# Gate copies issued in quarters between U tiles, and one U tile split in every step

## The chip, the cores and the metric

The kernel runs on one core of one Trainium2 chip. The metric is device time in microseconds (us) of one launch; lower is better. TensorE is called PE here, VectorE DVE, ScalarE ACT, GpSimd POOL. SP (SyncE) computes nothing: it issues DMAs.

## The reference, cut to what matters

One residual block over 512 tokens of width 1024: a gated token mixer, then a retrieval layer (PEER), then a norm. The change lies in the kernel's PEER part:

```
def peer(xn, w_q, sub_keys, u_tab, v_tab):       # 512 tokens, 8 heads, 128 x 128 = 16384 experts
    ...                                          # two top-16 searches per head, then the best 16 of the sums:
    ...                                          # idx (expert numbers) and g (softmax gates), 128 per token
    def block(args):                             # 128 tokens at a time
        tb, ib, gb = args
        ue = u_tab[ib]
        act = jax.nn.gelu(jnp.einsum("phkd,pd->phk", ue, tb))
        ve = v_tab[ib]
        return jnp.einsum("phk,phkd->pd", gb * act, ve)
```

So each token meets 128 chosen rows of U and of V, each weighted by its gate.

## The kernel before, in words

The kernel runs in stages on one core: the input projection and the mixers (to about 330 us of the span), the queries and the top-16 searches (to about 580), the gates (to about 855) and a V stretch to the end.

For the first 128 tokens the kernel gathers the chosen rows of U and V. For the other three groups of 128 tokens (the index `t_` in the code, 0 to 2) it computes densely: all 16384 hidden values, each multiplied by its gate, which is zero for an expert not chosen. The experts are cut into 128 tiles of 128. A U tile is 512 KB: it is loaded to `raw`, split into a high part `hi` (ACT) and a low part `lo` (DVE), multiplied with the tokens' high and low parts in 24 matmuls (`h_mm`, L147 to L149), and put through gelu (`h_act`). Of the 128 U tiles, 60 are worked through before the V stretch, as company for other work; results for which there is no room are written to HBM.

The gates stage makes, for each group of 128 tokens, a table `stg` of 128 x 128 x 128 gates in SBUF. It takes eight steps a group (here s0 to s7; `s2` in the code). In each step `mid()` does, for two sets of eight tokens, the gate products on PE (`gate_mm`, 32 matmuls into four PSUM tiles, of which there are six), their eviction to `stg` on ACT (L731, four a step), and on DVE the one-hot operands of the next step (`one_hot`, L716 and L718, four operations a step). Around it, `h_step` carries one U tile along: it asks for a load, takes loaded tiles from the list `raws` and makes their `hi` ahead of `mid()` and their `lo` behind it, so that they join the list `nxt`; then it multiplies the first tile of `nxt` and evicts it. `nxt` holds at most three tiles (`SB`), `raws` six buffers (`RB`). The argument `splits` says how many tiles the step splits at most.

There is one `stg` buffer. Groups 0 and 1 are copied from it to the table `gd` in HBM, four DMAs of 2 MB on SP's queue, and `h_step` then runs six times without gates (here b0 to b5, `HB`). Group 2 stays in SBUF. After it the kernel multiplies the last tile that is split, and the V stretch begins.

The order of instructions on PE, DVE, ACT and POOL is that of the code here: `pinned()` ties each to the one before it on its engine. It does so for every engine but SP (L93), whose order is left to the scheduler of the framework.

Of the kernel before, what the change touches and what calls it, by code (L numbers as in the profile page):

```python
# [25 lines left out]
NDT = NTT - 1  # L26
# [15 lines left out]
HB = (6, 6, 0)  # L42
# [5 lines left out]
GSTEP = (1, 0, 0)  # L48
SB = 3
# [11 lines left out]
def tile_block(ctx: ExitStack, tc: tile.TileContext, x, w_in, vecs, w_ax, w_out, n2row, w_q, skT,  # L61
# [12 lines left out]
    def ps_b(name):  # L74
        return ps.tile([P, 512], F32, tag="b", name=name, bufs=6)
# [22 lines left out]
    def load(src, name, nsub=None):  # L98
        raw = strm.tile([P, D], F32, tag="raw", name=f"raw_{name}", bufs=RB)
        dst = raw if nsub is None else raw.rearrange("p (a b) -> p a b", a=nsub)  # L100
        sync.dma_start(dst, src)
        return raw

    def split(raw, name, lo_eng, pl=None):
        hi = (pl or strm).tile([P, D], F32R, tag="hi", name=f"hi_{name}", bufs=SB)
        lo = (pl or strm).tile([P, D], F32R, tag="lo", name=f"lo_{name}", bufs=SB)
        act.activation(hi, raw, AF.Copy)  # L107
        lo_eng.tensor_tensor(lo, raw, hi, op=ALU.subtract)  # L108
        return hi, lo
# [45 lines left out]
    with ExitStack() as fctx:  # L155
# [31 lines left out]
        with pinned():  # L187
# [5 lines left out]
            raws = [load(w_in[s_ * KD], f"in{s_}_0") for s_ in (0, 1, 4)]  # L193
# [182 lines left out]
    def drain(left):  # L376
        while len(dq) > left:
            dq.pop(0)()
# [44 lines left out]
    def flush():  # L423
        while pend:
            h_act(*pend.pop(0))

    def h_load():
        nonlocal hn
        if hn < nlag:
            raws.append((hord[hn], load(uT[hord[hn]], f"u{hord[hn]}")))  # L430
            hn += 1

    def h_split(pl=None, lo_eng=pool, most=3):
        here = sum(1 for e in nxt if e[2] is None)
        if here < most - (pl is not None):
            pl = None
        elif pl is None or len(nxt) - here >= 3:
            return
        if raws:
            i, raw = raws.pop(0)  # L440
            nxt.append((i, split(raw, f"u{i}", lo_eng, pl), pl))

    def h_run():
        if nxt:
            i, (hi, lo), _ = nxt.pop(0)
            pend.append((i, h_mm(i, hi, lo)))

    raws, nxt = [], []

    def h_turn(n, lo_eng=pool):  # L450
        for _ in range(n):
            if len(raws) < 2:
                h_load()
            h_run()
            h_split(lo_eng=lo_eng)
            flush()
# [215 lines left out]
    def gather_steps(n, left=0):  # L672
        while n > 0 and gpos[0] < len(gsched):
            f, a = gsched[gpos[0]]
            f(a)
            drain(left)
            gpos[0] += 1
            if f is not gather_w:
                n -= 1
# [3 lines left out]
    with ExitStack() as gctx:  # L683
        op = gctx.enter_context(tc.tile_pool(name="op", bufs=1))
        io = op.tile([P, P, 2], F16, name="io")
        pool.iota(io, pattern=[[1, P], [0, 2]], base=0, channel_multiplier=0, allow_small_or_imprecise_dtypes=True)
        h_turn(HPRO)
        pte = ps_b("pte")
        ptg = ps_b("ptg")
        for t in range(NDT):  # L690
            pe.transpose(pte[:, t * P:(t + 1) * P], eall[:, 1 + t, :], ident)
            pe.transpose(ptg[:, t * P:(t + 1) * P], gall[:, 1 + t, :], ident)
        ef = op.tile([P, TD], F32, name="ef")
        ij = op.tile([P, TD // OC, 2, OC], F16, name="ij")
        g12 = op.tile([P, TD // OC, 2, OC], F16, name="g12")

        def by_sub(tl):
            return tl[:, :TD].rearrange("p (s o) -> p s o", o=OC)


        dve.tensor_scalar(ef, pte[:, :TD], 1.0 / NKEY, -(NKEY - 1.0) / (2 * NKEY), op0=ALU.mult, op1=ALU.add)
        act.activation(g12[:, :, 0, :], by_sub(ptg), AF.Copy, scale=GSC)
        dve.tensor_scalar(ef, ef, ROUND, -ROUND, op0=ALU.add, op1=ALU.add)
        dve.scalar_tensor_tensor(ij[:, :, 1, :], by_sub(ef), -float(NKEY), by_sub(pte), op0=ALU.mult, op1=ALU.add)
        act.activation(ij[:, :, 0, :], by_sub(ef), AF.Copy)
        dve.scalar_tensor_tensor(g12[:, :, 1, :], by_sub(ptg), GSC, g12[:, :, 0, :], op0=ALU.mult, op1=ALU.subtract)

        iob = io.unsqueeze(1).to_broadcast([P, OC, P, 2])

        def one_hot(sub):  # L710
            def bc(tl):
                pairs = tl[:, sub].rearrange("p v (q b) -> p (v q) b", b=2)
                return pairs.unsqueeze(2).to_broadcast([P, OC, P, 2])

            oij, o12 = [op.tile([P, OC, P, 2], F16, tag=n, name=f"{n}_{sub}", bufs=OB) for n in ("oij", "o12")]
            dve.tensor_tensor(oij, iob, bc(ij), op=ALU.is_equal)  # L716
            oi = oij[:, :OC // 2].unsqueeze(1).to_broadcast([P, 2, OC // 2, P, 2])
            dve.tensor_tensor(o12.rearrange("p (v q) k b -> p v q k b", v=2), oi,  # L718
                              bc(g12).rearrange("p (v q) k b -> p v q k b", v=2), op=ALU.mult)
            return oij, o12  # L720

        def gate_mm(sub, oij, o12):
            for q4 in range(OC // 4):
                pg = ps_b(f"pg{sub}_{q4}")
                for t in range(4):
                    o = pg[:, t * P:(t + 1) * P]
                    q, b = divmod(q4 * 4 + t, 2)
                    pe.matmul(o, oij[:, OC // 2 + q, :, b], o12[:, q, :, b], start=True, stop=False)
                    pe.matmul(o, oij[:, OC // 2 + q, :, b], o12[:, OC // 2 + q, :, b], start=False, stop=True)
                tt = sub * OC % P + q4 * 4  # L730
                act.activation(stg[:, :, tt:tt + 4], pg.rearrange("p (t i) -> p i t", t=4), AF.Copy)  # L731

        def h_step(mid, splits=1):
            if len(raws) < RB:
                h_load()
            made = []
            while len(made) < splits and len(nxt) + len(made) < SB and raws:
                k_, raw = raws.pop(0)  # L740
                hi = strm.tile([P, D], F32R, tag="hi", name=f"hi_u{k_}", bufs=SB)
                act.activation(hi, raw, AF.Copy)  # L742
                made.append((k_, raw, hi))
            mid()
            for k_, raw, hi in made:
                lo = strm.tile([P, D], F32R, tag="lo", name=f"lo_u{k_}", bufs=SB)
                dve.tensor_tensor(lo, raw, hi, op=ALU.subtract)  # L747
                nxt.append((k_, (hi, lo), None))
            h_run()
            flush()  # L750

        NSUB = NDT * P // OC
        ohs = {u: one_hot(u) for u in range(OB)}
        h_turn(HPRO2, dve)
        for t_ in range(NDT):
            stg = sp.tile([P, P, P], F32, tag="stg", name=f"stg{t_}", bufs=1)
            for s2 in range(P // OC // 2):
                sub = t_ * (P // OC) + 2 * s2

                def mid():  # L760
                    for u in (sub, sub + 1):
                        gate_mm(u, *ohs.pop(u))
                    for u in (sub + OB, sub + OB + 1):
                        if u < NSUB:
                            ohs[u] = one_hot(u)

                if s2 >= 4 and len(raws) < RB:
                    h_load()

                h_step(mid, 0 if t_ and s2 < 2 else 2 if s2 in (4, 6) else 1)  # L770
                gather_steps(GSTEP[(sub // 2) % len(GSTEP)], 2)
            if t_ < NDT - 1:
                for q4 in range(4):
                    sl = slice(q4 * 32, (q4 + 1) * 32)
                    sync.dma_start(gd[sl, :, t_ * P:(t_ + 1) * P].rearrange("i j t -> j i t"), stg[:, sl, :])  # L775
            for m in range(HB[t_]):
                h_step(lambda: None)
        while nxt or raws:
            flush()
            h_split()  # L780
            h_run()
        drain(0)
        flush()
# [54 lines left out]
    for i in range(NKEY):  # L838
        raw = vr.pop(i) if i in vr else load(v_tab[i * P:(i + 1) * P, :], f"v{i}")
        hi, lo = split(raw, f"v{i}", dve)  # L840
# [79 lines left out]
```

## Time and profile before

| | us |
|---|---|
| median of 3 runs | 1696.33 (1694.04 to 1698.31) |
| the profiled execution | 1695.04 |
| its span, first to last instruction | 1693.3 |
| PE busy | 1627.9 (96%) |
| DVE busy | 1267.5 (75%) |
| ACT busy | 690.1 (41%) |
| granted PE clock, mean over the span | 0.98 |

Times within the profile are counted from the span's start. A row of idle time names what ended it. The clock is the share of full speed that was granted to PE. Busy time of an engine that is not the bottleneck costs nothing by itself.

### The profile page before, as it was taken

The numbers are of one execution on the slowest core, as the hardware profiler recorded it, in microseconds if no ns is written. First come the engines' busy times: TensorE is split into PE (matmuls) and PEld (weight loads), VectorE is DVE, ScalarE is ACT, GpSimd is POOL, SyncE is SP. The second block draws the span as 40 slices with busy tenths as digits, with TensorE's granted clock in tenths as the row PEclk, the third lists the DMA queues.
The fourth block names the chain that finished last, engine by engine and source line by source line (L and its number), as shares of the span: only waits on it lengthen the run. The fifth ranks groups of instructions, "written<-read, shape, count | busy, mean of one in ns | idle before, by whom it ended". The sixth has DMA issues, their size and how long they took to land.

```text
span 1693.3 us, 23571 instructions
## 1 busy us (share of the span) xinstructions
PE 1627.9 (96%) x8402; PEld 1429.3 (84%) x8402; DVE 1267.5 (75%) x2404; ACT 690.1 (41%) x1222; POOL 501.3 (30%) x379
## 2 busy tenths in 40 slices
PE   9999999999999997696799999999999999999997
PEld 8888888888999997696798888998999888778886
DVE  6666666647999992664678888888888887877776
ACT  6444444434333452342443333333333343333334
POOL 0000000006888700000024454445444445221221
PEclk9999999999999998798899999999999999999999
DMA  6223332334333539176189999999999999988884
GB/s 219 90 90 103 107 103 90 97 125 142 119 119 111 187 124 321 61 234 215 55 277 320 324 322 330 316 335 330 334 338 326 324 332 337 346 292 307 292 302 145
DMA packets 157878, 378.31 MB, mean 223 GB/s; under 512 B 14016, under 2 KB 78016, under 8 KB 157632
## 3 DMA queue, kind: packets, MB, share of 16 engines
q1 hardware_dynamic: 112544, 229.86, 39.7%
q0 software_dynamic: 36864, 134.23, 22.6%
q10 hardware_dynamic: 8352, 12.72, 2.0%
q8 instruction: 65, 1.06, 0.3%
q14 instruction: 53, 0.43, 0.1%
HBM read 345.17 MB, written 31.59 MB: 223 GB/s over the span
## 4 chain that ended last, share of the span: by engine, by line
PE 76%; DMA 8%; DVE 7%; SPq 3%; issue 3%; ACT 2%; POOL 1%; DVEq 0%; ACTq 0%; POOLq 0%
PE acc L830 8%; PE acc L833 8%; PE acc L829 8%; PE ph L149 8%; PE ph L147 8%; PE ph L148 8%; PE pin L149 6%; PE pin L148 6%; PE pin L147 6%; SPq L775 3%; DMA rv<-in_v_tab_dram,eix 2%; DMA raw_u<-in_uT_dram 2%; DMA ru<-in_u_tab_dram,eix 2%; PE pq L147 2%; PE pq L148 2%
## 5 line engine op out<-in xcount | busy, mean ns | idle before, releaser
L149 PE MATMUL ph<-a1h,lo_u 128*128 128x384 f32 x1024 | 350.9, 343 | 27.0 <-DVE lo_u L747 26.5
L147 PE MATMUL ph<-a1h,hi_u 128*128 128x384 f32 x1024 | 352.5, 344 | 1.1 <-ACT hi_u L742 1.1
L148 PE MATMUL ph<-a1l,hi_u 128*128 128x384 f32 x1024 | 348.5, 340 | 0.0
L830 PE MATMUL acc<-lo_v,wh 128*128 128x512 f32 x768 | 303.6, 395 | 5.3 <-DVE lo_v L108 5.3
L829 PE MATMUL acc<-hi_v,wh 128*128 128x512 f32 x768 | 303.7, 396 | 0.0
L833 PE MATMUL acc<-hi_v,wl 128*128 128x512 f32 x768 | 242.8, 395 | 0.0
L364 POOL DMA_INDIRECT rv<-in_v_tab_dram,eix x128 | 159.4, 1246 | 281.5 <-ACT eix L669 204.8
L364 POOL DMA_INDIRECT ru<-in_u_tab_dram,eix x120 | 162.6, 1355 | 248.5 <-ACT eix L669 209.0
L387 DVE SCALAR_TENSOR_TENSOR acc<-rv,w,acc 128x1024 f32<-128x1024 f32 x128 | 164.7, 1286 | 86.8 <-DMA rv<-in_v_tab_dram,eix 84.4
L149 PEld LDWEIGHTS ph<-a1h,lo_u 128*128 128x128 f32 x1024 | 197.3, 193 | 29.4 <-DVE lo_u L747 28.5
L107 ACT ACTIVATE hi_v<-raw_v 128x1024 fp32r<-128x1024 f32 x128 | 134.9, 1055 | 189.5 <-PE ph L148 184.8
L147 PEld LDWEIGHTS ph<-a1h,hi_u 128*128 128x128 f32 x1024 | 197.6, 193 | 5.2 <-ACT hi_u L742 2.0
L373 DVE SCALAR_TENSOR_TENSOR ru<-ru,t 128x1024 f32<-128x1024 f32 x128 | 155.3, 1222 | 61.1 <-DMA ru<-in_u_tab_dram,eix 57.9
L148 PEld LDWEIGHTS ph<-a1l,hi_u 128*128 128x128 f32 x1024 | 197.1, 192 | 3.2
L849 ACT ACTIVATE wh<-wf 128x384 fp32r<-128x384 f32 x128 | 67.1, 525 | 275.4 <-PE acc L830 201.7
L830 PEld LDWEIGHTS acc<-lo_v,wh 128*128 128x128 f32 x768 | 144.0, 188 | 40.3 <-DVE lo_v L108 9.1
L149 PE MATMUL pin<-a1h,lo_in 128*128 128x512 f32 x448 | 174.4, 389 | 0.3 <-POOL lo_in L108 0.3
L148 PE MATMUL pin<-a1l,hi_in 128*128 128x512 f32 x448 | 174.4, 389 | 0.0
L147 PE MATMUL pin<-a1h,hi_in 128*128 128x512 f32 x448 | 174.3, 389 | 0.0
L833 PEld LDWEIGHTS acc<-hi_v,wl 128*128 128x128 f32 x768 | 144.0, 187 | 35.1
L829 PEld LDWEIGHTS acc<-hi_v,wh 128*128 128x128 f32 x768 | 143.9, 187 | 32.2 <-ACT hi_v L107 0.2
L108 DVE TENSOR_TENSOR lo_v<-raw_v,hi_v 128x1024 fp32r<-128x1024 f32 x128 | 156.0, 1219 | 2.7 <-ACT hi_v L107 2.6
(199 smaller groups left out, 2477.8 us busy)
## 6 DMA issues: line engine op xcount, KB each, us to landing
raw_u<-in_uT_dram SPq DMA_DIRECT2D x128, 512.0 KB
raw_v<-in_v_tab_dram SPq DMA_DIRECT2D x128, 512.0 KB
raw_in<-in_w_in_dram SPq DMA_DIRECT2D x56, 512.0 KB
gd<-stg SPq DMA_DIRECT2D x8, 2048.0 KB
gt<-gd SPq DMA_DIRECT2D x128, 128.0 KB
hd<-hg ACTq DMA_DIRECT2D x54, 192.0 KB
hr<-hd SPq DMA_DIRECT2D x54, 192.0 KB
raw_q<-in_w_q_dram SPq DMA_DIRECT2D x16, 512.0 KB
```

The lines of the kernel that those rows point to most:

```text
L107: act.activation(hi, raw, AF.Copy)
L108: lo_eng.tensor_tensor(lo, raw, hi, op=ALU.subtract)
L147: pe.matmul(pt, wh(k), xh(k), start=start and m == 0, stop=False)
L148: pe.matmul(pt, wh(k), xl(k), start=False, stop=False)
L149: pe.matmul(pt, wl(k), xh(k), start=False, stop=stop and m == n - 1)
L364: ins = pool.indirect_dma_start(out=rows, out_offset=None, in_=tab, in_offset=bass.IndirectOffsetOnAxis(ap=ix, axis=0))
L373: dq.append(lambda: dve.scalar_tensor_tensor(rows, rows, 1.0, t0, op0=ALU.mult, op1=ALU.mult, accum_out=d0[:, n:n + 1]))
L387: dq.append(lambda: dve.scalar_tensor_tensor(acc0, rows, w0[:, n:n + 1], acc0, op0=ALU.mult, op1=ALU.add))
L829: pe.matmul(accs[t][h], wh[:, ts], hi[:, hsl], start=first, stop=False)
L830: pe.matmul(accs[t][h], wh[:, ts], lo[:, hsl], start=False, stop=False)
L833: pe.matmul(accs[t][h], wl[:, ts], hi[:, hsl], start=False, stop=last)
L849: act.activation(wh, wf, AF.Copy)
```

## The change

The step loses its argument: every step splits one tile if there is room, where before s0 and s1 of groups 1 and 2 split none and s4 and s6 up to two. The four copies of a group, which stood in a row ahead of the plain steps, are each written ahead of one of the first four plain steps, whose load is written right behind.

```diff
-        def h_step(mid, splits=1):
+        def h_step(mid):
             if len(raws) < RB:
                 h_load()
-            made = []
-            while len(made) < splits and len(nxt) + len(made) < SB and raws:
+            made = None
+            if len(nxt) < SB and raws:
                 k_, raw = raws.pop(0)
                 hi = strm.tile([P, D], F32R, tag="hi", name=f"hi_u{k_}", bufs=SB)
                 act.activation(hi, raw, AF.Copy)
-                made.append((k_, raw, hi))
+                made = k_, raw, hi
             mid()
-            for k_, raw, hi in made:
+            if made:
+                k_, raw, hi = made
                 lo = strm.tile([P, D], F32R, tag="lo", name=f"lo_u{k_}", bufs=SB)
                 dve.tensor_tensor(lo, raw, hi, op=ALU.subtract)
                 nxt.append((k_, (hi, lo), None))
...
-                h_step(mid, 0 if t_ and s2 < 2 else 2 if s2 in (4, 6) else 1)
+                h_step(mid)
                 gather_steps(GSTEP[(sub // 2) % len(GSTEP)], 2)
-            if t_ < NDT - 1:
-                for q4 in range(4):
-                    sl = slice(q4 * 32, (q4 + 1) * 32)
+            for m in range(HB[t_]):
+
+                if m < 4:
+                    sl = slice(m * 32, (m + 1) * 32)
                     sync.dma_start(gd[sl, :, t_ * P:(t_ + 1) * P].rearrange("i j t -> j i t"), stg[:, sl, :])
-            for m in range(HB[t_]):
                 h_step(lambda: None)
```

`HB` is (6, 6, 0), so group 2 has no plain steps and no copies, as before.

## Rows read from the trace of the kernel before

**Rows 1.** The page: busy time of the engines, then from the span cut into 40 slices the busy tenths of PE and its granted clock in tenths.

```profile
PE 1627.9 (96%) x8402; PEld 1429.3 (84%) x8402; DVE 1267.5 (75%) x2404; ACT 690.1 (41%) x1222; POOL 501.3 (30%) x379
...
PE   9999999999999997696799999999999999999997
...
PEclk9999999999999998798899999999999999999999
```

**Rows 2.** Busy time by stretch: group 0's gate steps (from their first gates to the end of s7's evictions), its plain steps, group 1's gate steps, its plain steps, group 2's gate steps with the last U tile, the V stretch. Columns: stretch, its length, busy us and instructions of each engine, granted clock, DMA share and GB/s.

```profile
584.38:633.10 48.72, 47.92 (x444) 46.65 (x444) 47.53 (x42) 28.00 (x48) 3.04 (x3) 1.00 0.46 152
634.07:658.95 24.88, 24.88 (x145) 24.72 (x144) 8.11 (x7) 8.26 (x11) 0.00 (x0) 1.00 1.02 314
658.95:742.22 83.27, 58.74 (x450) 55.72 (x450) 48.89 (x44) 29.15 (x49) 1.87 (x2) 0.82 0.45 148
742.22:767.06 24.84, 24.84 (x145) 24.68 (x144) 9.12 (x9) 8.27 (x11) 1.68 (x1) 1.00 1.03 312
767.06:855.05 87.99, 64.45 (x473) 61.56 (x473) 51.50 (x51) 30.66 (x52) 0.94 (x1) 0.83 0.40 137
855.05:1690.00 834.95, 824.26 (x3937) 715.04 (x3936) 671.97 (x987) 323.83 (x671) 327.01 (x252) 1.00 0.89 313
```

**Rows 3.** The same columns for single steps, each from the start of its gates: one of group 0; then of group 1 s0 with s1, s2, s3, s4 and s5; then of group 2 s0 with s1, s2, s3, s4 and s6.

```profile
597.51:603.59 6.08, 6.08 (x57) 5.92 (x57) 5.59 (x6) 3.50 (x6) 0.00 (x0) 1.00 0.38 120
...
658.95:684.76 25.81, 15.00 (x113) 14.26 (x113) 11.81 (x11) 6.27 (x11) 0.73 (x1) 0.74 0.70 242
684.76:697.42 12.66, 8.08 (x57) 7.43 (x57) 5.95 (x5) 3.50 (x6) 0.21 (x1) 0.87 0.34 100
697.42:710.53 13.11, 8.54 (x58) 7.88 (x57) 5.95 (x5) 3.50 (x6) 0.00 (x0) 0.74 0.15 55
710.53:723.86 13.33, 8.76 (x57) 8.10 (x57) 8.23 (x8) 4.44 (x7) 0.94 (x1) 0.74 0.40 122
723.86:729.94 6.08, 6.08 (x57) 5.92 (x57) 4.87 (x5) 3.50 (x6) 0.00 (x0) 1.00 0.16 61
...
767.06:791.13 24.07, 14.47 (x113) 13.73 (x113) 10.67 (x9) 6.27 (x11) 0.00 (x0) 0.79 0.76 263
791.13:805.07 13.94, 9.36 (x58) 8.71 (x57) 7.09 (x7) 3.50 (x6) 0.94 (x1) 0.76 0.27 89
805.07:818.88 13.81, 9.24 (x58) 8.58 (x57) 5.95 (x5) 3.50 (x6) 0.00 (x0) 0.75 0.16 53
818.88:832.60 13.72, 8.93 (x57) 8.46 (x57) 7.08 (x6) 4.33 (x7) 0.00 (x0) 0.75 0.23 76
838.67:844.75 6.08, 6.08 (x57) 5.92 (x57) 6.01 (x7) 4.33 (x7) 0.00 (x0) 1.00 0.28 86
```

**Rows 4.** What PE waited for between 620 and 860 us (us in total, times, longest), and from the order of time four of PE's instructions with the idle time before each and what ended it: the first and the later half of group 1's s1 gates, the first matmul on lo_u in s2, the first gates of group 2's s1.

```profile
PE ph L149 <- DVE lo_u L747: 26.5, 6, 4.8
PE pg L728 <- DVE o L718: 20.4, 4, 10.3
...
675.49 0.29 PE L728 MATMUL pg<-o,oij 128*128 128x128 f16 x1 [10.30 <-DVE o L718]
677.89 0.29 PE L728 MATMUL pg<-o,oij 128*128 128x128 f16 x1 [0.51 <-DVE o L718]
691.97 0.69 PE L149 MATMUL ph<-a1h,lo_u 128*128 128x384 f32 x1 [4.38 <-DVE lo_u L747]
...
782.39 0.29 PE L728 MATMUL pg<-o,oij 128*128 128x128 f16 x1 [9.09 <-DVE o L718]
```

**Rows 5.** The turn from group 0 to group 1 in order of time (start, length, instruction; consecutive ones of a kind are one row): on SP the four copies and the seven loads behind them, then ACT.

```profile
632.10 23.39 SPq L775 DMA_DIRECT2D gd<-stg  x4
655.58 17.81 SPq L101 DMA_DIRECT2D raw_u<-in_uT_dram  x7
...
670.73 1.06 ACT L742 ACTIVATE hi_u<-raw_u 128x1024 fp32r<-128x1024 f32 x1 [15.25 <-DMA raw_u<-in_uT_dram]
672.62 2.06 ACT L731 ACTIVATE stg<-pg 128x512 f32<-128x512 f32 x4 [0.46 <-ACT hg L404]
```

**Rows 6.** DVE in order of time: two lo's of the end of group 0; in group 1 the first operation of the one-hots that s2's gates read, the last one, then the lo that s2 itself waits for; in group 2 a gather's sum, at the end of s5.

```profile
634.84 1.22 DVE L747 TENSOR_TENSOR lo_u<-raw_u,hi_u 128x1024 fp32r<-128x1024 f32 x1
...
640.34 1.23 DVE L747 TENSOR_TENSOR lo_u<-raw_u,hi_u 128x1024 fp32r<-128x1024 f32 x1 [2.88 <-ACT hi_u L742]
...
677.75 1.22 DVE L716 TENSOR_TENSOR oij<-io,ij 128x2048 f16<-128x2048 f16 x1
...
681.39 1.23 DVE L718 TENSOR_TENSOR o<-oij,g 128x2048 f16<-128x2048 f16 x1
...
690.70 1.22 DVE L747 TENSOR_TENSOR lo_u<-raw_u,hi_u 128x1024 fp32r<-128x1024 f32 x1
...
839.66 1.22 DVE L373 SCALAR_TENSOR_TENSOR ru<-ru,t 128x1024 f32<-128x1024 f32 x1
```

**Rows 7.** SP's issues early in the span, in order of time: n2b, and the loads of the queries' stage up to sks.

```profile
16.21 1.30 SPq L304 DMA_DIRECT2D n2b<-in_n2row_dram  x1
...
333.91 23.86 SPq L101 DMA_DIRECT2D raw_q<-in_w_q_dram  x5
383.79 0.33 SPq L595 DMA_DIRECT2D sks<-in_skT_dram  x1
```

**Rows 8.** Busy time while group 0's copies are under way, with the columns of rows 2.

```profile
632.00:668.00 36.00, 33.19 (x213) 32.72 (x211) 10.15 (x9) 8.33 (x12) 0.08 (x1) 1.00 0.98 295
```

## The prediction

> **What bounds the kernel now.** I read the page first: TensorE (PE) is busy 96% of the span, so time is only to be had where PE stands still or runs slowly. The row of PE's busy tenths and the row of its clock fall together in one place, slices 16 to 20, some 635 to 847 us [rows 1]. That is the stage of the gates, about 584 to 855 us, where the diff is too.
>
> Next I cut that stage by group of tokens, with a row for each group's eight gate steps (s0 to s7) and for the six plain steps behind them (b0 to b5) [rows 2]. Group 0's eight steps have PE busy 47.92 of 48.72 us at full clock. Both rows of plain steps are solid: 24.88 and 24.84 us, no idle time. But group 1's gate steps take 83.27 us with 58.74 busy at clock 0.82, and group 2's, with the last U tile behind them, 87.99 with 64.45 at 0.83. The long V stretch after that is busy 824.26 of 834.95 us.
>
> Then the same by single step [rows 3]. A step of group 0 takes 6.08 us, all of it PE. In group 1, s0 and s1 take 25.81 together, s2, s3 and s4 take 12.66, 13.11 and 13.33, and s5 is back at 6.08. Group 2 has the same picture: 24.07, then 13.94, 13.81 and 13.72, and 6.08 again in s6.
>
> So there are two kinds of loss. The waits of PE tell them apart [rows 4]. One wait per group, 10.30 and 9.09 us, stands before the gates of s1. Six more, up to 4.8 us each and 26.5 in all, stand before the first matmul that reads lo_u (L149), the first at 691.97, in s2.
>
> The first kind has its cause in the queue [rows 5]: group 0's four copies are issued between 632.10 and 655.5 us, the loads behind them only after that. ScalarE (ACT) therefore waits 15.25 us for the raw tile of b5, and VectorE (DVE), in order, holds that tile's lo, then the one-hots of s1, behind it.
>
> The second kind has its cause in the list of prepared tiles. Counting it through the loop by hand: the splits that s0 and s1 leave out take it from two tiles to none, so that s2 splits the very tile it multiplies. Its lo stands on DVE behind two one-hots and begins at 690.70 [rows 6], and PE waits until 691.97. s3 does the same. s4 splits two, but its own product again needs the first of them; only from s5 on is there one ahead.
>
> **The change, part by part.**
>
> *Every step splits one tile.* Group 0 is untouched: there the double split of s4 and s6 finds no room in the list (three tiles at most, two already in it). In groups 1 and 2 the list now stays at two, as in group 0, and s2 to s4 become steps of its kind, 6.08 us [rows 3]. Group 1: 12.66 + 13.11 + 13.33 - 3 x 6.08 = 20.86. Group 2: 13.94 + 13.81 + 13.72 - 3 x 6.08 = 23.23. Sum 44.09 us.
>
> Not all of that is waiting: the six waits on lo_u sum to 26.5 us [rows 4], and most of the other 17.6 is matmuls at a clock of 0.74 to 0.87 [rows 3]. The Trainium skill has the rule, in "TensorE: Matmul & The Clock Gate", section "Why this matters for your kernels": no idle gaps of PE over some 3 us, one window of idle brings half rate. The trace agrees: the gap of 4.38 us that ends at 691.97 [rows 4] is in a step whose clock is 0.87, and the next has 0.74. By waits alone, without that rule, the sum would be 26.5 us instead of 44. By the same rule the wait of 9 to 10 us that stays would still bring the half rate behind it.
>
> What the splits cost where they go to: in s0 one hi (1.06 us) now stands on ACT ahead of the evictions that began at 672.62, and one lo (1.22) on DVE between the one-hots of s1 and those of s2, at 677.75 [rows 5, 6]. Cover on ACT: the four evictions end at 674.68, and the gates of s1 that need their PSUM come at 677.89 [rows 4, 5], 3.2 us later. Cover on DVE: the one-hots of s2 end at 682.62, the gates that read them start at 684.76 (where s2's row begins [rows 3]), 2.1 us for 1.22. So I cost it at nothing; uncovered it is 2.28 us a group, 4.6 in all. Their loads: the queue has issued them before it comes to its next wait (seven by 673.4 [rows 5]), and 512 KB at 242 GB/s, the mean of s0 and s1, takes 2.2 us, against 6.08 for a step.
>
> A step now always has DVE busy for some 5.9 of 6.08 us [rows 3]. Five of the sixteen steps add a gather's sum of 1.22 us [rows 6], and DVE would be late by that. The nearest row is group 2's s6, which starts with such a sum at 839.66 and still takes 6.08 [rows 3, 6], since the second one-hot is read only halfway through the gates. I take 0; the upper end is 5 x 1.22 = 6.1 us. Below nothing isn't to be had: no work is removed.
>
> The loads of group 1's later steps come earlier than now. Those steps have a DMA share of 0.15 to 0.40 [rows 3], so this costs nothing.
>
> *Copies one by one, a load behind each.* In the code the order is now copy, load, copy, load. What SP issues need not be that. The kernel pins the order of the other engines and leaves SP out (L93), and the trace shows SP's orders moved: the load of n2b (L304), which the code calls behind all eight rounds of the first stage, is issued at 16.21 us, and that of sks (L595), called behind two loads of w_q, at 383.79, behind five of them [rows 7]. Both stand where they were ready, not where they are written. All four copies become ready together, when the last eviction is done at about 632; the load of b0 needs the raw buffer that DVE frees with the lo that starts at 634.84 [rows 5, 6]. A queue filled by readiness gives the four copies first, then the loads: today's order. I take this as the likelier, and cost the part at nothing. In that case the first wait of each group stays: 10.30 and 9.09.
>
> **Sum.** The profiled execution took 1695.04 us (1693.3 of span); less 44.09 that is 1650.95. The median of the runs shown is 1.3 us above it. The stretch behind is PE-bound (824.26 of 834.95 [rows 2]) with work of its own, so the gain should come through whole.
>
> **Rivals.**
>
> *The quarters do alternate on the queue.* Then the tile of b5 is there in time and DVE makes the one-hots of s1 early, but the evictions of s0 write the tile that the copies read and wait for the last copy. Today that one lands no later than 670.73 less one load: 512 KB at 295 GB/s [rows 8] is 1.8 us, so 669. Three loads ahead of it add 5.3 us: 674.3. Two of s1's four PSUM tiles are free (six in all, four in s0), so half of its gates run at once. The other half needs the first eviction done (four take 2.06 us [rows 5], so 0.5) and begins at 674.8, where today it begins at 677.89 [rows 4]. That is 3 us a group, 6 in all: 1645. If the loads cost the copies nothing, 5.3 a group more: 1634; if they cost twice as much, the first wait grows by 2.3 a group: 1656. For it: the code's order. Against it: the rows on readiness.
>
> *A new bound takes part of it.* The uncovered splits and late sums above, 4.6 and 6.1 us, together 1662; if a group's wait in s1 also grew by what two more loads take (3.6 us each group), 1669. For it: DVE's slack of less than 0.2 us in a step. Against it: group 2's s6.
>
> *Slower.* The last copy lands so late that the evictions of s0 hold PE longer than the three short waits did. From the rows: s2 may begin 20.86 us later than today before group 1 loses, so the first eviction would have to come at about 693 instead of 672.62 and the last copy land 22 us behind 669. The way to it is a copy that stands on SP behind loads that wait for their buffers. In the written order the last copy stands behind the load of b2, whose buffer is freed with the lo that starts at 640.34 [rows 6], when the first copies are still under way; for a loss it would have to be behind the load that follows b5. If it did and the copies ran 30 us late, the price is 8 us a group, 1711.
>
> *No change.* The V stretch, at a DMA share of 0.89 [rows 2], gives it back, because it starts with less loaded. It can't swallow 44 us that way: six raw buffers of 512 KB at 313 GB/s are 10 us. About 1660 then. No change at all needs a mechanism that I don't see in the rows.
>
> **Chances.** Forecast (today's queue, 44 us) 0.60; alternating quarters 0.24; a new bound, 1662 to 1669, or the V stretch, 1660, 0.07; no change 0.04; slower 0.05. Time: 1651. The range 1637 to 1662 holds the first two with their bounds but for the far end of the second, and the near part of the third. A measurement of this kernel can tell about 0.3%, 5 us, from no change; so faster 0.91, same 0.04, slower 0.05.
>
> **What the profile after should show.** Steps s2 to s4 of groups 1 and 2 at about 6.08 us with clock 1.0 from s3 on; no wait of L149 for lo_u in them. The wait before s1's gates still 9 to 10 us, with the four copies ahead of the loads on SP; 6 to 8 us and loads between the copies if the rival holds. V stretch 835 us as now. I am wrong if the waits on lo_u are still there under another name (one-hots of DVE, hi of ACT), or if the V stretch is longer by what the gates save.

## Result and the profile after

The changed kernel takes 1641.01 us (1639.71 to 1642.99, four runs), the kernel before 1697.32 beside it: ratio 0.9678, 95% interval [0.9665, 0.9691], so 3.2% faster. The profiled execution took 1639.71 us, 55.3 us less than that of before.

The page of the kernel after, the rows that answer to [rows 1]: busy time, and over 40 slices PE's busy tenths and its clock.

```profile
PE 1610.1 (98%) x8402; PEld 1415.1 (86%) x8402; DVE 1266.4 (77%) x2404; ACT 689.4 (42%) x1222; POOL 515.2 (31%) x379
...
PE   9999999999999999898999999999999999999997
...
PEclk9999999999999999999999999999999999999999
```

The dent of slices 16 to 20 is almost gone. Busy time by stretch, in the columns of [rows 2]: group 1 with its plain steps, group 2 with the last U tile, the V stretch; then single steps as in [rows 3]: of group 1 s0 with s1, s2, s3, s4; of group 2 the same.

```profile
658.45:740.24 81.79, 75.56 (x594) 74.12 (x593) 58.09 (x52) 37.36 (x60) 4.30 (x3) 0.96 0.78 244
740.24:801.83 61.59, 55.11 (x473) 53.65 (x473) 51.66 (x55) 29.83 (x52) 1.68 (x1) 0.94 0.60 195
801.83:1636.00 834.17, 823.82 (x3937) 714.59 (x3936) 669.53 (x983) 323.02 (x670) 339.31 (x252) 1.00 0.89 313
...
658.45:678.73 20.28, 14.05 (x113) 13.62 (x113) 13.12 (x12) 7.01 (x12) 0.00 (x0) 0.83 1.01 315
678.73:684.81 6.08, 6.08 (x57) 5.92 (x57) 4.87 (x5) 3.50 (x6) 0.94 (x1) 1.00 0.61 199
684.81:690.89 6.08, 6.08 (x57) 5.92 (x57) 5.95 (x6) 3.50 (x6) 0.00 (x0) 1.00 0.37 119
690.89:696.97 6.08, 6.08 (x57) 5.92 (x57) 5.95 (x6) 3.50 (x6) 0.00 (x0) 1.00 0.35 121
...
740.24:760.43 20.19, 14.22 (x114) 13.78 (x113) 11.98 (x10) 7.01 (x12) 0.00 (x0) 0.83 1.03 328
760.43:766.51 6.08, 6.08 (x58) 5.92 (x57) 4.88 (x5) 3.50 (x6) 0.00 (x0) 1.00 0.28 107
766.51:772.59 6.08, 6.08 (x58) 5.92 (x57) 6.01 (x7) 3.51 (x6) 1.68 (x1) 1.00 0.51 160
772.59:778.73 6.14, 6.14 (x58) 5.92 (x57) 6.07 (x6) 3.39 (x6) 0.00 (x0) 1.00 0.37 132
```

Group 1 with its plain steps took 83.27 + 24.84 = 108.11 us before [rows 2], now 81.79: 26.3 less. Group 2 went from 87.99 to 61.59: 26.4 less. The V stretch, counted to the end of the span, went from 838.2 to 836.1, and what lies ahead of group 1 is 0.5 us shorter. Together 55.3.

Within the groups: s2 to s4 gave 20.9 and 23.2 us, as summed. s0 with s1 gave 5.5 and 3.9 more (25.81 to 20.28, 24.07 to 20.19 [rows 3]); that is the part that the forecast had left out.

Where it comes from is seen at the turn to group 1, which answers to [rows 5]: SP's issues, the lo on DVE that frees the buffer of the first load, ACT's evictions of s0, then PE's first gates of s1, its wait ahead of their later half and the same wait in group 2. Idle time and what ended it stand in brackets.

```profile
631.60 0.38 SPq L776 DMA_DIRECT2D gd<-stg  x1
635.58 4.04 SPq L101 DMA_DIRECT2D raw_u<-in_uT_dram  x1
639.67 1.17 SPq L776 DMA_DIRECT2D gd<-stg  x1
640.94 7.93 SPq L101 DMA_DIRECT2D raw_u<-in_uT_dram  x1
648.92 1.20 SPq L776 DMA_DIRECT2D gd<-stg  x1
650.22 8.76 SPq L101 DMA_DIRECT2D raw_u<-in_uT_dram  x1
659.03 1.07 SPq L776 DMA_DIRECT2D gd<-stg  x1
...
634.34 1.22 DVE L748 TENSOR_TENSOR lo_u<-raw_u,hi_u 128x1024 fp32r<-128x1024 f32 x1
...
671.21 2.06 ACT L731 ACTIVATE stg<-pg 128x512 f32<-128x512 f32 x4 [10.54 <-DMA gd<-stg]
...
664.53 0.24 PE L728 MATMUL pg<-o,oij 128*128 128x128 f16 x1
...
671.86 0.27 PE L728 MATMUL pg<-o,oij 128*128 128x128 f16 x1 [6.23 <-ACT stg L731]
...
753.39 0.27 PE L728 MATMUL pg<-o,oij 128*128 128x128 f16 x1 [5.97 <-ACT stg L731]
```

Copies and loads do alternate. The first load starts at 635.58, when the lo ends that frees its buffer (634.34 + 1.22); until then SP stands ahead of it, with three copies behind it that have been ready since the last eviction. ACT no longer waits for a raw tile; it waits for the last copy. PE's wait of 10.30 us for a one-hot [rows 4] has become one of 6.23 for an eviction, and half of s1's gates now run before it.

### The profile page after: what moved, and what is told of

Its sections match the earlier page's. It is cut to its first block, busy times and chain, and to the rows that moved or that the text cites. A ratio compares the mean times of both kernels' runs of the same rounds, so it can differ in the third digit from the quotient of the medians.

```text
span 1637.9 us, 23565 instructions
## 1 busy us (share of the span) xinstructions
PE 1610.1 (98%) x8402; PEld 1415.1 (86%) x8402; DVE 1266.4 (77%) x2404; ACT 689.4 (42%) x1222; POOL 515.2 (31%) x379
## 3 DMA queue, kind: packets, MB, share of 16 engines
q0 software_dynamic: 36864, 134.23, 23.2%
## 4 chain that ended last, share of the span: by engine, by line
PE 73%; issue 8%; DVE 7%; DMA 6%; POOL 4%; ACT 1%; SPq 0%; POOLq 0%; DVEq 0%; ACTq 0%
PE ph L147 9%; PE ph L149 9%; PE ph L148 9%; PE pin L149 6%; PE pin L147 6%; PE pin L148 6%; PE acc L830 6%; PE acc L833 6%; PE acc L829 6%; POOL rv L364 3%; DMA rv<-in_v_tab_dram,eix 3%; PE pq L147 2%; PE pq L149 2%; PE pq L148 2%; DMA gd<-stg 1%
## 5 line engine op out<-in xcount | busy, mean ns | idle before, releaser
L147 PE MATMUL ph<-a1h,hi_u 128*128 128x384 f32 x1024 | 347.1, 339 | 0.0
L149 PE MATMUL ph<-a1h,lo_u 128*128 128x384 f32 x1024 | 344.1, 336 | 0.4 <-POOL lo_u L108 0.4
L148 PE MATMUL ph<-a1l,hi_u 128*128 128x384 f32 x1024 | 343.3, 335 | 0.0
L364 POOL DMA_INDIRECT rv<-in_v_tab_dram,eix x128 | 170.3, 1331 | 271.2 <-ACT eix L669 230.8
L148 PEld LDWEIGHTS ph<-a1l,hi_u 128*128 128x128 f32 x1024 | 193.1, 189 | 3.2
L147 PEld LDWEIGHTS ph<-a1h,hi_u 128*128 128x128 f32 x1024 | 193.1, 189 | 3.1
L149 PEld LDWEIGHTS ph<-a1h,lo_u 128*128 128x128 f32 x1024 | 192.8, 188 | 0.7 <-POOL lo_u L108 0.7
L149 PE MATMUL pin<-a1h,lo_in 128*128 128x512 f32 x448 | 174.4, 389 | 0.3 <-POOL lo_in L108 0.3
```

What stands on the lines that cost most here:

```text
L147: pe.matmul(pt, wh(k), xh(k), start=start and m == 0, stop=False)
L148: pe.matmul(pt, wh(k), xl(k), start=False, stop=False)
L149: pe.matmul(pt, wl(k), xh(k), start=False, stop=stop and m == n - 1)
L364: ins = pool.indirect_dma_start(out=rows, out_offset=None, in_=tab, in_offset=bass.IndirectOffsetOnAxis(ap=ix, axis=0))
```

## Experiments

The theory after the result: the two parts add up. The splits are worth the 44 us of s2 to s4. The order of the queue takes some 10 us off the first waits, because the tile of b5 and so the one-hots of s1 are there in time. What is left of the first wait is the evictions of s0 waiting for the last copy.

### The splits alone

The kernel before, with the one line changed; the copies stay in a row.

```diff
-                h_step(mid, 0 if t_ and s2 < 2 else 2 if s2 in (4, 6) else 1)
+                h_step(mid)
```

> One part alone: every step splits one tile, the four copies stay in a row ahead of the plain steps. Theory: the two parts add up, and this one is worth the 44.1 us worked out from s2 to s4; profiled time about 1651, s2 to s4 of groups 1 and 2 at 6.08 us, the waits before s1's gates still 9 to 10 us, nothing of L149 waiting for lo_u. Rival: with the copies ahead of all loads, the splits put back into s0 and s1 make ACT wait for loads that are late, and the evictions behind it hold PE; then the first wait grows to 12 us or more a group and the time is 1658 or more. Second rival: it is the order of copies and loads that did most of it; then 1680 or more.

Measured: 1649.67 us, ratio to before 0.9732 [0.9711, 0.9753]. What PE waited for between 620 and 860 us is one kind (total, times, longest). The rows behind it are ACT's wait for the tile of b5, PE's first wait, and s0 with s1, then s2 and s3, of group 1.

```profile
PE pg L728 <- DVE o L718: 20.7, 5, 10.1
...
670.18 1.06 ACT L742 ACTIVATE hi_u<-raw_u 128x1024 fp32r<-128x1024 f32 x1 [15.08 <-DMA raw_u<-in_uT_dram]
...
674.95 0.29 PE L728 MATMUL pg<-o,oij 128*128 128x128 f16 x1 [10.12 <-DVE o L718]
...
658.58:684.08 25.50, 14.87 (x114) 14.13 (x113) 12.67 (x11) 8.05 (x13) 0.00 (x0) 0.73 0.76 265
684.08:690.16 6.08, 6.08 (x58) 5.92 (x57) 6.01 (x7) 3.50 (x6) 1.68 (x1) 1.00 0.68 205
690.16:696.24 6.08, 6.08 (x58) 5.92 (x57) 6.01 (x7) 3.50 (x6) 0.00 (x0) 1.00 0.36 121
```

This is the case that I had forecast, and it came out at its 1651 within 2 us. L149 waits for no lo_u any more. The splits put back into s0 and s1 cost nothing: s0 with s1 take 25.50 us, 25.81 before. Both rivals fall.

### The quarters alone

The kernel before, with the copies moved and the old splits:

```diff
-            if t_ < NDT - 1:
-                for q4 in range(4):
-                    sl = slice(q4 * 32, (q4 + 1) * 32)
+            for m in range(HB[t_]):
+                if m < 4:
+                    sl = slice(m * 32, (m + 1) * 32)
                     sync.dma_start(gd[sl, :, t_ * P:(t_ + 1) * P].rearrange("i j t -> j i t"), stg[:, sl, :])
-            for m in range(HB[t_]):
                 h_step(lambda: None)
```

> The other part alone: copies one by one ahead of the first four plain steps, but s0 and s1 of groups 1 and 2 still split none and s4 and s6 up to two. Theory: only the first wait of each group shrinks, as it did with both parts (s0 and s1 took 5.5 and 3.9 us less), so 9 to 10 us in all, profiled time about 1686; the six waits of L149 on lo_u of 4.3 us or more are still there, with a clock below 1.0 in s2 to s4. Rival: the list ran empty only because loads came late, and with loads in time the steps without a split cost little; then most of the 55 us is here, 1655 or less.

Measured: 1685.06 us, ratio 0.9939 [0.9921, 0.9957]. PE's waits between 620 and 860 us, and s2, s3 and s4 of group 1:

```profile
PE ph L149 <- DVE lo_u L747: 26.4, 6, 4.8
PE pg L728 <- ACT stg L731: 13.1, 2, 6.7
...
678.93:691.64 12.71, 8.13 (x58) 7.48 (x57) 5.95 (x5) 3.50 (x6) 0.00 (x0) 0.87 0.30 99
691.64:704.87 13.23, 8.66 (x58) 8.01 (x57) 5.95 (x5) 3.50 (x6) 0.00 (x0) 0.74 0.15 54
704.87:718.29 13.42, 8.85 (x57) 8.19 (x57) 8.23 (x8) 4.44 (x7) 0.94 (x1) 0.75 0.38 129
```

The six waits on lo_u are those of [rows 4], 26.4 us against 26.5, though the loads now come in time. So the list ran empty by the order of the code, and not because loads came late. From the ratios the splits alone are worth 45 us, the quarters alone 10, both 55: they add up.

### Copies written late

Both parts, but all four copies are written together ahead of b3. This asks what sets SP's order.

```diff
-                if m < 4:
-                    sl = slice(m * 32, (m + 1) * 32)
+                for q4 in range(4 if m == 3 else 0):
+                    sl = slice(q4 * 32, (q4 + 1) * 32)
```

> Both parts, but all four copies are written together ahead of the fourth plain step (b3). Theory that SP issues in the written order: three loads, then four copies, the first copy not before the lo of b1 (some 10 us later than now), the first wait longer by about that, time some 15 us above 1640. Theory that SP is filled by readiness, with each copy holding the queue's place for a while: the first copy still goes out at the last eviction, 631 to 632 us, ahead of loads that are written before it, the others between the loads; time within 5 us of 1640.

Measured: 1642.94 us (a single time). SP at the turn to group 1:

```profile
631.85 0.38 SPq L775 DMA_DIRECT2D gd<-stg  x1
635.83 4.89 SPq L101 DMA_DIRECT2D raw_u<-in_uT_dram  x2
640.78 1.21 SPq L775 DMA_DIRECT2D gd<-stg  x1
643.76 8.37 SPq L101 DMA_DIRECT2D raw_u<-in_uT_dram  x1
652.18 7.82 SPq L775 DMA_DIRECT2D gd<-stg  x2
```

The first copy goes out at the last eviction, ahead of three loads written before it, so the written order doesn't bind. But the copies don't go out in a row either: two loads come ahead of the second. Nor is this the order in which things become ready in the trace: the last eviction frees all four copies at 631.85, and the load behind the first copy starts only at 635.83, with three ready copies behind it. So the second theory holds for the first copy and for the time, but readiness does not explain the rest. What sets the order between a load and a copy can't be seen in a trace; it stays open.

### Two more U tiles beside the copies

Both parts, eight plain steps for six; four U tiles move there from the V stretch.

```diff
-SPILL = 54
+SPILL = 58
...
-HB = (6, 6, 0)
+HB = (8, 8, 0)
```

> Both parts, and eight plain steps instead of six behind groups 0 and 1 (HB 8, 8, 0); the four U tiles for it are taken from the V stretch (SPILL 58 instead of 54), so PE's work is the same. Theory: what is left of the first wait (6.23 and 5.97 us) is the evictions of s0 waiting for the last copy, which lands at a fixed time behind s7; two more U tiles, 8.3 us, cover it. s0 with s1, 20.3 and 20.2 us now, come down to about 12.2, so 16 us in all, profiled time about 1624. Rival: the wait has another cause (PSUM, one-hots) and moves along: 1638 to 1642. Second rival: four more results written to HBM and read back cost the V stretch as much as the gates gain, DMA being busy 0.89 there: 1635 or more with the first wait gone.

Measured: 1631.24 us, ratio to before 0.9627 [0.9604, 0.965], which doesn't overlap with that of the changed kernel. It is the faster of the two by some 9 us (8.6 by the ratios, 9.8 by the medians), where I had expected 16. Of what is missing, 4.0 us are the two waits that stayed, 2.27 and 1.76. ACT at the turn to group 1, PE's wait ahead of the later half of s1's gates, and that stretch up to the start of s2:

```profile
674.75 1.06 ACT L742 ACTIVATE hi_u<-raw_u 128x1024 fp32r<-128x1024 f32 x1 [7.16 <-DMA raw_u<-in_uT_dram]
675.72 2.04 ACT L731 ACTIVATE stg<-pg 128x512 f32<-128x512 f32 x4
...
676.35 0.22 PE L728 MATMUL pg<-o,oij 128*128 128x128 f16 x1 [2.27 <-ACT stg L731]
...
676.35:681.51 5.16, 5.16 (x40) 5.00 (x39) 5.09 (x5) 4.70 (x9) 0.00 (x0) 1.00 0.93 370
```

The wait shrank from 6.23 to 2.27 us, and no half clock follows it. What stands before the evictions now is not the copy but a raw tile: with eight plain steps the hi of s0 is that of the load behind the last copy.

### The hi of s0 behind the evictions

Like the kernel with two more U tiles, but with `hi` in s0 of groups 1 and 2 made after `mid()`.

```diff
-                act.activation(hi, raw, AF.Copy)
+                if not late:
+                    act.activation(hi, raw, AF.Copy)
...
+                if late:
+                    act.activation(hi, raw, AF.Copy)
```

> As the run with eight plain steps, but in s0 of groups 1 and 2 the hi of the split is made behind the evictions instead of ahead of them. Theory: of the first wait 2.27 and 1.76 us were left with eight plain steps, because ACT, in order, waited 7.2 us for the raw tile behind the last copy before it came to the evictions, which could have run some 4 us earlier; with the hi behind them the wait before s1's second half is gone in both groups, 4 us, plus up to 1 us of late one-hots behind it: 1626 against 1631. Rival: it is the last copy itself that the evictions wait for, in which case the wait and the time stay: 1630 to 1632.

Measured: 1631.14 us (1624.77 to 1635.59), ratio 0.9611 [0.9575, 0.9647]: no gain that can be told from the run before. ACT's evictions, then group 1's s0 with s1, s2 and s3:

```profile
672.02 2.06 ACT L731 ACTIVATE stg<-pg 128x512 f32<-128x512 f32 x4 [4.10 <-DMA gd<-stg]
674.97 1.06 ACT L749 ACTIVATE hi_u<-raw_u 128x1024 fp32r<-128x1024 f32 x1 [0.89 <-DMA raw_u<-in_uT_dram]
...
667.23:679.55 12.32, 12.32 (x113) 11.84 (x112) 8.46 (x8) 6.68 (x12) 0.00 (x0) 1.00 1.02 348
679.55:687.28 7.73, 6.24 (x56) 5.91 (x57) 7.66 (x9) 3.82 (x7) 1.68 (x1) 1.00 0.59 210
687.28:694.38 7.10, 6.28 (x58) 5.95 (x57) 7.00 (x7) 3.49 (x6) 0.00 (x0) 1.00 0.50 168
```

The mechanism was right and the forecast of the time wrong. The evictions come at 672.02 and s0 with s1 take 12.32 us, free of waiting. But the hi still comes at 674.97, its lo stands on DVE ahead of the next one-hots, and DVE has no slack to make it up: s2 and s3 take 7.73 and 7.10 us. The wait has only moved: the V stretch begins at 808.14 us, at 808.16 in the run before.

### One more U tile

Both parts with `HB = (7, 7, 0)` and `SPILL = 56`.

> Both parts with seven plain steps behind groups 0 and 1 (HB 7, 7, 0, SPILL 56). Theory: the evictions of s0 wait for the last copy, which lands at the same time (about 671.2 us) whatever runs beside it, so one U tile of 4.16 us takes that much from waits of 6.23 and 5.97 and leaves about 2; too short a gap to bring the half clock, so s0 with s1 take about 14.2 us: 1630 to 1632, about what eight steps gave. Rival: the last copy is put off by the additional load, the waits stay above 4 us: 1635 or more.

Measured: 1634.36 us (1631.71 to 1640.34), ratio 0.963 [0.9606, 0.9653]: between the two, 2 to 4 us above what I expected. ACT's evictions of s0 and PE's wait of group 1, then the stretches behind that wait in groups 1 and 2:

```profile
672.08 2.07 ACT L731 ACTIVATE stg<-pg 128x512 f32<-128x512 f32 x4 [5.86 <-DMA gd<-stg]
...
672.73 0.27 PE L728 MATMUL pg<-o,oij 128*128 128x128 f16 x1 [2.73 <-ACT stg L731]
...
672.73:679.38 6.65, 6.65 (x41) 6.49 (x40) 4.72 (x5) 4.80 (x9) 0.00 (x0) 0.76 0.96 371
...
755.22:763.17 7.95, 7.95 (x40) 7.79 (x39) 3.58 (x3) 4.81 (x9) 0.00 (x0) 0.62 0.99 377
```

The waits are 2.73 and 3.01 us (5.7 in all), more than the 2 that I took, and they do bring a half clock: the same work takes 6.65 and 7.95 us where, at full clock, it took 5.16 with eight steps. The rival, waits above 4 us, doesn't hold, though its cause is there on a small scale: the evictions begin at 672.08, against 671.21 with six steps.

## Why the prediction came out as it did

*What bounds the kernel:* right. All of the gain but 2.6 us lies in groups 1 and 2.

*Every step splits one tile, 44.09 us:* right in mechanism and size. s2 to s4 went to 6.08 us but for one of 6.14, and the part alone gave 45 us. That the sum counts the half clock and not only the waits was needed: 26.5 us of waits would have been far too little. What I had costed at nothing (the hi and lo in s0 and s1, DVE's lack of slack, the earlier loads) cost next to nothing: group 2 gained 26.4 us, 0.7 less than its steps s0 to s4, and 0.5 of that is one wait of PE for a one-hot in its last step.

*Copies one by one, costed at nothing:* this step failed. I took it as likelier that "a queue filled by readiness gives the four copies first, then the loads: today's order". SP issued copy, load, copy, load. Half of the premise stands by the copies written late: the written order doesn't bind. The other half, that readiness sets the order, does not: the second copy was ready at 631.6, the load issued ahead of it not before 635.56, and SP waited for that load. The second copy went out 8.1 us behind the first. The rows on n2b and sks [rows 7] showed only that SP can leave the written order, not what it goes by instead; that stays open.

*The rival with alternating quarters* is what happened, and its mechanism is right to the letter: one-hots early, half of s1's gates ahead, the rest behind the last copy. Its size was 6 us and was 9.4. The last copy had landed by 671.2, not 674.3. The copies' DMA packets in the two traces end at 667.2 us before and 670.8 after, 35.1 and 39.2 us behind the first copy's issue: my 669 was 1.8 us late, and with three loads in between the copies took 4.1 us longer, not the 5.3 that I took from the mean rate. And the gates' later half began at 671.86 against my 674.8.

*The rival Slower* has a wrong sum, which the result doesn't touch. By the working of the alternating quarters, the later half of s1's gates could begin 20.86 us behind today's 677.89, so the last copy could land at about 698, 29 us behind 669 and not 22. Copies 30 us late would have cost about 1 us in group 1, not 8 a group.

*V stretch with nothing given back:* right, 834.17 against 834.95 us in the window.

The time forecast, 1651, is that of the splits alone (1649.67); the 10 us between it and the result are the rival's, and lay within the range, which was laid to hold both.

## What to carry to other kernels

Where a software pipeline keeps a list of prepared tiles, count its length through every step, the irregular ones too: here two steps that prepared nothing were paid for in the three behind them, with PE's half clock on top. A transfer that a reused buffer waits for has a landing time of its own, so put as much independent PE work between its issue and the reuse as it takes to land, and see that no load needed meanwhile queues behind all of it. Don't bet on the order of a queue that the code doesn't pin: here neither the written order nor readiness in the trace gave it, so price both orders.

## What the runs showed of the hardware

A wait of 2.73 us was enough to bring PE's half clock (0.76 mean over the 6.65 us behind it), one of 3.01 too (0.62 over 7.95 us), and one of 2.27 brought none (1.00 over 5.16 us). The Trainium skill, "TensorE: Matmul & The Clock Gate", section "Why this matters for your kernels", puts the limit at gaps of some 3 us and an idle window; here a gap somewhat shorter did it. I had not expected it of so short a wait. The price of a short wait is therefore not its length: 2.73 us cost another 1.5, and 3.01 another 2.8.

Nor does the length of the wait give the length of the half clock. Two stretches at half clock with one more tile, behind the waits of 2.73 and 3.01 us, then two of the kernel before, with waits of 4.38 and 4.33 us:

```profile
672.57:675.98 3.41, 3.25 (x21) 3.25 (x21) 1.32 (x2) 2.95 (x7) 0.00 (x0) 0.50 0.90 350
754.49:761.32 6.83, 6.10 (x30) 6.10 (x30) 3.82 (x4) 5.45 (x10) 0.00 (x0) 0.50 1.02 383
...
691.82:695.24 3.42, 3.27 (x10) 3.27 (x11) 0.10 (x1) 0.00 (x0) 0.00 (x0) 0.50 0.48 153
702.06:708.89 6.83, 4.26 (x13) 4.26 (x14) 2.48 (x3) 0.00 (x0) 0.00 (x0) 0.50 0.20 77
```

Wherever the half clock came in the gates stage of these traces, it lasted a whole multiple of 3.41 us, up to 13.65. The second of these stretches began 2.28 us into its wait, where elsewhere a whole wait of 2.27 us brought none; so these runs give no limit for the length of a wait.

512 KB loads and 2 MB copies on one queue wait for each other. In the kernel before, the packets of the loads behind the four copies start at 666.26 us, as those of the copies come to their end (667.20); with the splits alone such a load left ACT waiting 15.08 us. With the copies one by one no raw tile was late with six plain steps, and the last copy ended 4.1 us later, counted from the issue of the first.
